# A hybrid conv/SSD and dilated-attention block pair in fp32: output scaling moved behind the hybrid projection, attention products regrouped

## The chip, the cores and the metric

The kernel runs on one core of one Trainium2 chip. The metric is device time in microseconds (us) of one execution. Data come in as fp32; no host arithmetic. A core's engines are TensorE (PE, with its weight loads as PEld), VectorE (DVE), ScalarE (ACT), GpSimd (POOL) and SyncE (SP, which issues the transfers here).

## The reference

A sequence of 256 tokens of width 1024 goes through two layers. Each layer is a half-step SwiGLU feed-forward block, a mixer, and another half-step feed-forward block, every one between two RMS norms. The mixer of layer 0 is a causal convolution joined with a state-space scan; that of layer 1 is attention over three patterns of eight heads.

```python
for i in range(DEPTH):
    h = h + 0.5 * rms_norm(swiglu(rms_norm(h, g[0]), w1[i, 0], w2[i, 0]), g[1])
    u = rms_norm(h, g[2])
    m = conv_ssd_mixer(u, ...) if i % 2 == 0 else dilated_attention_mixer(u, w_qkv, w_o)
    h = h + rms_norm(m, g[3])
    h = h + 0.5 * rms_norm(swiglu(rms_norm(h, g[4]), w1[i, 1], w2[i, 1]), g[5])

def conv_ssd_mixer(u, ...):
    conv_in, z, xbc, dt_raw = jnp.split(u @ w_in, [s0, s1, s2], axis=-1)
    ya = conformer_conv(conv_in, ...)      # 31-tap causal convolution, layer norm, silu
    yb = mamba2_ssd(z, xbc, dt_raw, ...)   # 4-tap convolution, chunked scan, silu(z) gate, rms_norm
    return jnp.concatenate([ya, yb], axis=-1) @ w_out

def dilated_attention_mixer(u, w_qkv, w_o):
    qkv = (u @ w_qkv).reshape(b, seq, 3, 3, 8, 64)
    for g, (window, dilation) in enumerate(((128, 1), (512, 4), (2048, 16))):
        o, l = dilated_window_attention(q[g], k[g], v[g], slopes, window, dilation)
        outs.append(o); lses.append(l)     # output and log-sum-exp of its scores, per group
    weights = softmax(stack(lses), axis=0)
    return einsum('gblh,gblhd->blhd', weights, stack(outs)).reshape(b, seq, 512) @ w_o
```

The norm at the end of `mamba2_ssd` divides each token's row by its root mean square over all 1024 channels and multiplies by a gain per channel. The merge of the three attention groups is a softmax over all three groups' scores at once.

## The kernel before, in words

Everything stays on the chip; tokens are two tiles (t = 0, 1) of 128 rows. Every dense product is done in three: a value is split into a high part rounded to the matmul's fp32r type and a low part (value minus high part), and hi x hi, hi x lo and lo x hi are added up in PSUM (`mm3`). Attention's scores and weighting are plain fp32 matmuls instead, which the trace and the order show as two passes each.

The 178 weight units of 1 MB come in one order (`_ffn_units`, `_hyb_units`, `_attn_units`): feed-forward 33 units (0 to 32), hybrid 26 (33 to 58), two feed-forward blocks, attention 20, feed-forward. `prefetch` runs three units ahead over four buffers each of `raw`, `wh`, `wl`: SP loads `raw`, ACT casts it to the high part `wh`, and DVE subtracts to get `wl`. For the units in `GPSIMD_UNITS` POOL does that subtraction instead, in pieces of `POOL_PIECE` columns, and ACT's cast is cut alike.

The hybrid stage computes the projections, DVE and ACT do the 31-tap convolution tap by tap, the scan works on PE with help from DVE, ACT and POOL, and its gated result sits in the tiles `v` (list `xs`, four of them, two halves per token tile). For each token tile `rstd` takes the row sums of squares, a power on POOL, and gives the row scale; the four v tiles are scaled on ACT, transposed on PE and split while they leave PSUM (`spread`, where the gain per channel is put in). Then the output projection collects in four PSUM banks `acc`: four units of products with the scan's part (`of_yb`), then four with the convolution's (`of_ya`).

The attention stage computes values of groups 0 and 1, then for each group q and k (feature-major, in `cv` tiles, both through the two "w" banks), the scores (64 features on one half of the array's rows per head, so that heads go in pairs on both halves), a running maximum and sum, and the exponentials. `weigh` for the group before transposes the probabilities (stationary operand, 128x128) and multiplies them with 64 columns of v; each group's output is added to `num`, rescaled by the change of the maximum. At the end `num` is divided by the sum, transposed, split and projected.

Every operation is recorded first (`Recorder`), and `schedule` then fixes the static order of each engine and the places of the buffers: among the operations that could start, by a modelled time (`cost`, `latency`), it takes the one of lowest rank, where the rank is the place in the program plus what `moved` adds. All operations are issued from one line, L423, so the profile's rows are told apart by tile names: wh and wl are a unit's high and low part, x transposed activations, a, w, t, c the four kinds of PSUM bank (4, 2, 1 and 1 of them), s scratch tiles in SBUF, cv the convolution's tiles and attention's q and k, v values, y0 and y1 half rows of 512, m small columns.

## Time and profile before

| what | value |
|---|---|
| three runs | 1132.56 us median, 1129.19 to 1132.75 |
| profiled execution | 1132.12 us, span 1130.3 us |
| PE busy | 1095.5 us of the span (97%), 5830 instructions |
| PEld, DVE, ACT, POOL busy | 919.5, 738.6, 635.2, 148.2 us |
| granted TensorE clock, mean | 0.993 |
| hybrid stage | from about 209 to 406 us |
| attention stage | from about 782 to 944 us |

Times in a view are us from the span's start. An instruction's row reads: its line, engine, operation, output <- inputs, shape and type, and its count. In a table of groups there follow the busy time, the mean of one in ns, and the idle time of the engine just before them with what ended it. The order of inputs in a PE row is moving operand first, stationary second. PE rows are pipelined, so that one's end runs on under the next; what a product costs on PE is read from start to start.

### The profile page before, as it was taken

The page shows a single profiled execution, that of the slowest core. Times are in us where ns is not written, and L with a number is a line of the kernel's source. Part 1 is how long each engine was busy: PE and PEld are TensorE (multiplying, and loading weights), DVE is VectorE, ACT ScalarE, POOL GpSimd, SP SyncE. Part 2 cuts the span into 40 slices and gives each one's busy share as a digit, 9 for nine tenths or more (in the row PEclk, how much of TensorE's full clock was granted, in tenths as well). Part 3 has the DMA queues.
Part 4 walks back from the last instruction along what each step waited for, and adds up shares of the span by engine and source line. Part 5 has one row for each costly group of instructions (what it writes and reads, how often), then busy time and mean ns, then how long its engine had stood idle before and what let it go on. Part 6 is the DMA issues. An engine that isn't in the chain of part 4 may idle for free.

```text
span 1130.3 us, 15336 instructions
## 1 busy us (share of the span) xinstructions
PE 1095.5 (97%) x5830; PEld 919.5 (81%) x5830; DVE 738.6 (65%) x1248; ACT 635.2 (56%) x1217; POOL 148.2 (13%) x200
## 2 busy tenths in 40 slices
PE   6999999999899999999999999999999999999997
PEld 5888888798767778888878888888877877888885
DVE  5756556799797685655686555667575657555563
ACT  7645545788667564554565454545565456455452
POOL 0000000379795300000010000001000000000000
PEclk9999999999999999999999999999999999999999
DMA  9755454534333466546546546554632424654521
GB/s 349 260 189 186 165 208 149 190 146 150 112 109 116 186 229 217 186 157 215 186 149 224 205 174 221 180 193 159 237 138 79 150 75 152 220 181 174 215 83 38
DMA packets 30203, 196.55 MB, mean 174 GB/s; under 512 B 3633, under 2 KB 4529, under 8 KB 7601
## 3 DMA queue, kind: packets, MB, share of 16 engines
q1 hardware_dynamic: 30128, 195.57, 48.9%
q8 instruction: 45, 0.74, 0.2%
q14 instruction: 30, 0.24, 0.1%
HBM read 194.51 MB, written 1.05 MB: 173 GB/s over the span
## 4 chain that ended last, share of the span: by engine, by line
PE 63%; DVE 4%; ACT 3%; POOL 3%; issue 1%; DVEq 0%; POOLq 0%; ACTq 0%
PE w L423 26%; PE a L423 22%; PE t L423 8%; PE c L423 7%; ACT s L423 1%; POOL wl L423 1%; ACT wh L423 1%; DVE y L423 1%; POOL s L423 1%; DVE wl L423 1%; DVE s L423 1%; POOL m L423 1%; DVE h L423 1%; DVE x L423 0%; DVE m L423 0%
## 5 line engine op out<-in xcount | busy, mean ns | idle before, releaser
L423 DVE TENSOR_TENSOR wl<-raw,wh 128x1024 fp32r<-128x1024 f32 (+1 forms) x322 | 385.1, 1220 | 215.6 <-ACT wh L423 214.0
L423 ACT ACTIVATE wh<-raw 128x1024 fp32r<-128x1024 f32 (+2 forms) x466 | 375.7, 854 | 232.4 <-PE a L423 91.5
L423 PE MATMUL w<-x,wh 128*128 128x512 f32 (+1 forms) x992 | 315.6, 373 | 3.5 <-DVE cv L423 2.1
L423 PE MATMUL w<-x,wl 128*128 128x256 f32 x880 | 247.9, 282 | 0.0
L423 PE MATMUL a<-wh,s 128*128 128x512 f32 x768 | 246.2, 395 | 0.0
L423 PEld LDWEIGHTS w<-x,wh 128*128 128x128 f32 x992 | 179.8, 189 | 40.2 <-DVE cv L423 3.1
L423 PEld LDWEIGHTS a<-wh,s 128*128 128x128 f32 x768 | 143.9, 188 | 34.7 <-DVE s L423 0.6
L423 PEld LDWEIGHTS w<-x,wl 128*128 128x128 f32 x880 | 166.9, 190 | 1.9 <-issue 0.6
L423 PE MATMUL w<-wh,x 128*128 128x512 f32 x480 | 159.3, 405 | 2.5 <-ACT x L423 2.5
L423 PE MATMUL a<-wl,s 128*128 128x512 f32 x384 | 151.8, 395 | 1.8 <-POOL wl L423 1.8
L423 POOL TENSOR_TENSOR m<-m,mhalf 128x1 f32<-128x1 f32 x28 | 19.6, 701 | 939.0 <-DVE m L423 939.0
L423 PEld LDWEIGHTS w<-wh,x 128*128 128x128 f32 x480 | 90.9, 191 | 24.6 <-ACT x L423 3.1
L423 POOL TENSOR_TENSOR wl<-raw,wh 128x256 fp32r<-128x256 f32 x144 | 103.7, 761 | 37.1 <-ACT wh L423 37.0
L423 PE MATMUL t<-x,wh 128*128 128x512 f32 x288 | 102.7, 396 | 0.0
L423 PE MATMUL c<-x,wh 128*128 128x512 f32 x288 | 102.7, 395 | 0.0
L423 PE MATMUL w<-wl,x 128*128 128x512 f32 x240 | 95.5, 400 | 1.7 <-POOL wl L423 1.7
L423 PEld LDWEIGHTS a<-wl,s 128*128 128x128 f32 x384 | 72.1, 188 | 17.6 <-POOL wl L423 2.2
L423 ACT ACTIVATE sg<-w 128x256 f32<-128x256 f32 x96 | 36.6, 382 | 86.7 <-PE w L423 86.6
L423 PE MATMUL t<-x,wl 128*128 128x256 f32 x288 | 80.8, 281 | 0.0
L423 PE MATMUL c<-x,wl 128*128 128x256 f32 x288 | 80.8, 281 | 0.0
L423 DVE TENSOR_TENSOR sg<-w,sg 128x256 f32<-128x256 f32 x72 | 30.3, 421 | 72.6 <-ACT sg L423 72.6
L423 PEld LDWEIGHTS t<-x,wh 128*128 128x128 f32 x288 | 54.0, 188 | 12.8
(167 smaller groups left out, 1211.3 us busy)
## 6 DMA issues: line engine op xcount, KB each, us to landing
raw<-in_weights SPq DMA_DIRECT2D x176, 1024.0 KB, 4.8
g<-in_gains SPq DMA_DIRECT2D x11, 512.0 KB, 4.7
raw<-in_weights SPq DMA_DIRECT2D x4, 256.0 KB, 6.1
raw<-in_weights SPq DMA_DIRECT2D x2, 512.0 KB, 7.9
out<-h SPq DMA_DIRECT2D x4, 256.0 KB, 2.1
s<-in_consts SPq DMA_DIRECT2D x3, 192.0 KB, 4.0
h<-in_x SPq DMA_DIRECT2D x2, 256.0 KB, 2.8
h<-in_x SPq DMA_DIRECT2D x1, 512.0 KB, 6.7
```

Source lines behind the costliest of these rows:

```text
L423: o.ins = f(*[real(a) for a in o.args], **{k: real(a) for k, a in o.kw.items()})
```

## The change

Hybrid stage. The v tiles are transposed and split without the row scale; the scale is kept (`rms`) and applied to the four PSUM accumulators, in place on ACT, when the scan's part of the projection is complete and before the convolution's part is added. POOL's pieces are 512 columns wide instead of 256, and unit 55 is split by DVE. In the planner, POOL's lengths are other numbers.

Attention stage. Group 2's values come first, those of groups 0 and 1 last. All three groups' scores are computed and exponentiated one after the other, with the products of a block put into one unbroken run by the new `together`; q goes through the "w" banks and k through "t" and "c". The probabilities of all groups are kept. `settle` brings those of groups 0 and 1 to the last maximum by multiplying them on POOL (12 tiles of 128x512 with a broadcast factor). `weigh` has v's 64 columns as the stationary operand and the transposed probabilities (128 columns) moving, heads by turns on the left and right half of the array's columns, and one accumulator per token tile takes all three groups. Evictions of transposed probabilities go to ACT and DVE by turns. The result is already transposed; the reciprocal sums are spread out and transposed instead (`spread`), multiplied in, and the product is split for the projection. Line 423 becomes line 439.

```diff
-POOL_PIECE = 256
+POOL_PIECE = 512
-GPSIMD_UNITS = range(38, 56)
+GPSIMD_UNITS = range(38, 55)
...
-SMALL = {1: 16, 2: 12, 8: 12, 12: 2, 16: 6, 32: 8}
+SMALL = {1: 16, 2: 12, 8: 28, 12: 2, 16: 6, 32: 8}
...
+    def together(self):
+        at = len(self.ops)
+        yield
+        head, rest = self.ops[at], self.ops[at + 1 :]
+        for o in rest:
+            for d, read in o.deps.items():
+                if d < at:
+                    head.deps[d] = head.deps.get(d, False) or read
...
+            o.rank = head.rank - RUN
+            o.deps.setdefault(o.index - 1, False)
...
+        if PAIRED and (stationary.ap.ap[0][1] == 64 or stationary.free_size() == 64):
+            return max(2 * n / 2.4 + 5.0, 110.0), 0.0
...
-        return (2.35 if out.ap.dtype == F32R else 1.9) * n + 40.0, 0.0
+        spread = any(isinstance(v, View) and v.ap.ap[-1][0] == 0 for v in kw.values())
+        return (1.95 if spread else 2.35) * n + (10.0 if spread else 92.0), 0.0
...
-            r = self.rstd(ss, EPS)
-            for g in range(2):
-                nc.scalar.activation(xs[t][g], xs[t][g], AF.Copy, scale=r)
+            rms.append(self.rstd(ss, EPS))
...
-                out_unit(of_yb, j, t, units[j], j == 0, False)
+                out_unit(of_yb, j, t, units[j], j == 0, j == 3)
+
+            for half in acc[t]:
+                nc.scalar.activation(half, half, AF.Copy, scale=rms[t])
...
+                for n, s in enumerate(probs[t][g]):
+                    i, r = n // 2, n % 2
+                    nc.gpsimd.tensor_tensor(out=s, in0=s, in1=fv[:, i * per : (i + 1) * per, r].unsqueeze(2).to_broadcast([P, per, (t + 1) * P]), op=ALU.mult)
...
+                if i % 2:
+                    V.tensor_copy(out=o, in_=ps)
                 else:
+                    nc.scalar.activation(o, ps, AF.Copy)
...
+                with nc.together():
+                    blocks = [divmod(n, nb) for n in range(4 * i, 4 * i + 8)]
+                    for kb in range(nb):
+                        for hd in sorted({hd for hd, _ in blocks}):
+                            n = hd * nb + kb
+                            out = po[t][(hd % 2) * 64 : (hd % 2) * 64 + 64, hd // 2, :]
+                            nc.tensor.matmul(out, v[kb][:, hd * 64 : (hd + 1) * 64], pT[n // 4][:, n % 4, :], start=g == 2 and kb == 0 and hd < 2, stop=g == 1 and kb == nb - 1 and hd >= 6)
...
+        v = values(2)
+        for g in range(3):
+            softmax(g, proj(0.125, "ww"), proj(1.0, "tc"))
+        rden = [settle(t) for t in range(NT)]
+        for t in range(NT):
+            weigh(2, t, v)
+        for g in range(2):
+            v = values(g)
+            for t in range(NT):
+                weigh(g, t, v)
+            if g == 0:
+                rden = [spread(t, rden[t]) for t in range(NT)]
```

The order of the engines, at three places. A row gives the line, the operation, output <- inputs (moving, stationary; the number at a name's end is the buffer's own), shape and count. First PE in the hybrid stage, where the products with unit 48 (wh_48, wl_48) go into accumulator a_22. Before:

```order
L423 MATMUL a_22_2945<-x_6_1718,wh_48_2822 128x256 x2
L423 MATMUL a_22_2945<-x_6_1718,wl_48_2860 128x256
L423 MATMUL a_22_2945<-x_6_1718,wh_48_2822 128x256 x2
L423 MATMUL w_36_2828<-wh_46_2581,x_7_1721 128x512
L423 MATMUL a_22_2945<-x_6_1718,wl_48_2860 128x256
L423 MATMUL a_22_2945<-x_7_1721,wh_48_2822 128x256 x2
L423 MATMUL w_36_2828<-wl_46_2645,x_7_1721 128x512
L423 MATMUL w_36_2828<-wh_46_2581,x_7_1721 128x512
L423 MATMUL a_22_2945<-x_7_1721,wl_48_2860 128x256
L423 MATMUL a_22_2945<-x_7_1721,wh_48_2822 128x256 x2
L423 MATMUL w_37_2989<-wh_45_2487,x_4_1710 128x512
L423 MATMUL a_22_2945<-x_7_1721,wl_48_2860 128x256
```

and now:

```order
L439 MATMUL a_22_2858<-x_5_1714,wh_48_2738 128x256 x2
L439 MATMUL a_22_2858<-x_5_1714,wl_48_2793 128x256
L439 MATMUL a_22_2858<-x_6_1718,wh_48_2738 128x256 x2
L439 MATMUL w_36_2747<-wl_46_2586,x_7_1721 128x512
L439 MATMUL w_36_2747<-wh_46_2516,x_7_1721 128x512
L439 MATMUL w_37_2885<-wh_45_2433,x_4_1710 128x512
L439 MATMUL w_37_2885<-wl_45_2520,x_4_1710 128x512
L439 MATMUL w_37_2885<-wh_45_2433,x_4_1710 128x512 x2
L439 MATMUL w_38_2895<-x_4_1710,wh_47_2661 128x256 x2
L439 MATMUL w_38_2895<-x_4_1710,wl_47_2725 128x256
L439 MATMUL w_38_2895<-x_4_1710,wh_47_2661 128x256 x2
L439 MATMUL w_38_2895<-x_4_1710,wl_47_2725 128x256
```

The products of a_22 were mixed with three of w_36. Now a_22 stops in its third quarter of channels (x_6), and two products of w_36, four of w_37 and 24 of w_38 (wh_47, wl_47, in rows like the last four to x_7) come before the first one that reads wl_48 again.

Second, PE where the transposes of v begin and the scan's part of the output projection (a_35, a_36 with unit 51) follows. Before:

```order
L423 MATMUL w_41_3223<-wh_50_3064,x_7_1721 128x512 x2
L423 MATMUL w_41_3223<-wl_50_3072,x_7_1721 128x512
L423 MATMUL w_43_3435<-ident_0_70,cv_13_2832 128x128 x2
L423 MATMUL w_43_3435<-ident_0_70,cv_14_2853 128x128 x2
L423 MATMUL w_41_3223<-wh_50_3064,x_7_1721 128x512
L423 MATMUL w_44_3466<-ident_0_70,v_0_2891 128x128 x4
L423 MATMUL w_45_3476<-ident_0_70,v_2_3184 128x128 x4
L423 MATMUL a_35_3489<-wh_51_3138,x_8_3482 128x512
L423 MATMUL a_35_3489<-wl_51_3165,x_8_3482 128x512
L423 MATMUL a_36_3498<-wh_51_3138,x_8_3482 128x512
```

and now:

```order
L439 MATMUL w_41_3246<-wh_50_3001,x_6_1718 128x512
L439 MATMUL w_44_3307<-ident_0_70,v_0_2807 128x128 x4
L439 MATMUL w_41_3246<-wh_50_3001,x_7_1721 128x512
L439 MATMUL w_41_3246<-wl_50_3013,x_7_1721 128x512
L439 MATMUL w_41_3246<-wh_50_3001,x_7_1721 128x512 x2
L439 MATMUL w_41_3246<-wl_50_3013,x_7_1721 128x512
L439 MATMUL w_41_3246<-wh_50_3001,x_7_1721 128x512
L439 MATMUL a_35_3330<-wh_51_3036,x_8_3318 128x512
L439 MATMUL a_35_3330<-wl_51_3071,x_8_3318 128x512
L439 MATMUL a_36_3336<-wh_51_3036,x_8_3318 128x512
L439 MATMUL a_36_3336<-wl_51_3071,x_8_3318 128x512
L439 MATMUL a_35_3330<-wh_51_3036,x_8_3318 128x512
```

The first transposes of v (w_44) came after the last product of w_41 (the z gate) and with those of w_45; now w_44 stands five rows of w_41 earlier, and w_45 and w_46 between the projection's products.

Third, PE in the attention stage, scores of the first group's second half of heads (cv_36 to cv_38) into the banks a_47 to a_52. Before:

```order
L423 MATMUL w_108_7525<-x_20_7100,wh_133_7360 128x512
L423 MATMUL w_108_7525<-x_20_7100,wl_133_7371 128x256
L423 MATMUL w_108_7525<-x_20_7100,wh_133_7360 128x512
L423 MATMUL w_108_7525<-x_20_7100,wl_133_7371 128x256
L423 MATMUL w_108_7525<-x_21_7104,wh_133_7360 128x512
L423 MATMUL w_108_7525<-x_21_7104,wl_133_7371 128x256
L423 MATMUL a_51_7541<-cv_38_7482,cv_36_7388 128x256 x2
L423 MATMUL w_108_7525<-x_21_7104,wh_133_7360 128x512
L423 MATMUL w_108_7525<-x_21_7104,wl_133_7371 128x256
L423 MATMUL w_108_7525<-x_22_7108,wh_133_7360 128x512
L423 MATMUL a_52_7554<-cv_38_7482,cv_36_7388 128x256 x2
```

and now:

```order
L439 MATMUL a_47_7303<-cv_38_7260,cv_36_7166 128x128
L439 MATMUL a_48_7305<-cv_38_7260,cv_36_7166 128x128
L439 MATMUL a_47_7303<-cv_38_7260,cv_36_7166 128x128
L439 MATMUL a_48_7305<-cv_38_7260,cv_36_7166 128x128
L439 MATMUL w_102_7287<-x_21_6952,wl_131_7149 128x256
L439 MATMUL w_102_7287<-x_22_6956,wh_131_7138 128x512
L439 MATMUL a_51_7321<-cv_38_7260,cv_36_7166 128x256
L439 MATMUL a_52_7324<-cv_38_7260,cv_36_7166 128x256
L439 MATMUL a_51_7321<-cv_38_7260,cv_36_7166 128x256
L439 MATMUL a_52_7324<-cv_38_7260,cv_36_7166 128x256
L439 MATMUL w_102_7287<-x_22_6956,wl_131_7149 128x256
L439 MATMUL w_102_7287<-x_22_6956,wh_131_7138 128x512
```

The two 256-wide products on a_51 stood together, and those on a_52 four projection products later; now a_51 and a_52, on the two halves of the array's rows, go by turns without a break.

More of the change, by code (lines that the diff above doesn't have):

```diff
@@ L428 @@
 GAP = 100.0
+PAIRED = True
 FIRST = 730.0
@@ new lines, in spread @@
+        def spread(t, r):
+            wide = self.slot([P, 8, 64], tag="cv")
+            nc.scalar.activation(wide, r.unsqueeze(2).to_broadcast([P, 8, 64]), AF.Copy)
+            wide = wide.rearrange("p h c -> p (h c)")
+            ps = self.ps([P, 4, P], "tc"[t])
+            for b in range(4):
+                nc.tensor.transpose(ps[:, b, :], wide[:, b * P : (b + 1) * P], self.ident)
+            out = self.slot([P, 4, P], tag=f"y{t}")
+            nc.scalar.activation(out, ps, AF.Copy)
+            return out
```

191 lines of the change are left out of this document (91 added, 100 removed).

## The prediction

> **What bounds the kernel now.** I read the stage windows first, then the waits of TensorE (PE) in the two stages that the diff touches, then the single gaps, then the groups by shape. The other four stages are the two half-steps' feed-forward work, which the diff leaves alone. The stages read: start:end, length, then busy time and count of PE, PEld, DVE, ACT and POOL, the granted clock, the DMA share and GB/s.
>
> ```profile
> 209.00:406.00 197.00, 185.19 (x1082) 155.22 (x1081) 163.59 (x394) 136.79 (x346) 133.38 (x174) 0.98 0.41 146
> ...
> 594.00:782.00 188.00, 187.77 (x961) 157.66 (x960) 118.10 (x163) 99.05 (x160) 3.04 (x4) 1.00 0.55 193
> 782.00:944.00 162.00, 155.63 (x909) 130.37 (x908) 102.52 (x198) 93.72 (x223) 3.03 (x4) 0.99 0.38 136
> ```
>
> A feed-forward stage (second row) has PE busy for 187.8 of 188 us. The hybrid stage (first row) leaves it 11.8 us idle, the attention stage (third) 6.4. DMA is busy for 0.41 and 0.38 of the time, so weights arrive in time in both. PE is the bound, and time can only come from its idle time, its clock, and what its instructions cost. POOL, idle elsewhere, works 133 of 197 us in the hybrid stage. PE's waits there (total, times, longest):
>
> ```profile
> PE a L423 <- POOL wl L423: 4.6, 2, 2.8
> PE w L423 <- ACT v L423: 2.4, 1, 2.4
> PE w L423 <- POOL wl L423: 1.7, 1, 1.7
> ...
> PE a L423 <- POOL s L423: 0.8, 1, 0.8
> ```
>
> and in the attention stage:
>
> ```profile
> PE w L423 <- DVE cv L423: 2.1, 1, 2.1
> PE t L423 <- ACT s L423: 1.3, 2, 1.0
> ```
>
> The long ones in the timeline of PE (start, length, work, and in brackets the idle time before it), and, last, two products in undisturbed work:
>
> ```profile
> 295.77 0.49 PE L423 MATMUL a<-x,wl 128*128 128x256 f32 x1 [2.81 <-POOL wl L423]
> ...
> 343.12 0.55 PE L423 MATMUL w<-ident,v 128*128 128x128 f32 x3 [2.41 <-ACT v L423]
> ...
> 375.87 0.50 PE L423 MATMUL a<-wl,s 128*128 128x512 f32 x1 [1.80 <-POOL wl L423]
> ...
> 872.19 0.50 PE L423 MATMUL w<-x,wh 128*128 128x512 f32 x1 [2.14 <-DVE cv L423]
> ...
> 818.12 0.39 PE L423 MATMUL w<-x,wh 128*128 128x512 f32 x1
> 818.35 0.28 PE L423 MATMUL w<-x,wl 128*128 128x256 f32 x1
> ```
>
> From start to start a 512-wide product takes 0.23 us; half as wide is 0.12.
>
> A long gap costs twice. Of the four windows of 3.40 us below, three start right behind the gaps of 2.81, 2.41 and 2.14 us, and the last lies in undisturbed work; the third number from the end is the granted clock.
>
> ```profile
> 295.90:299.30 3.40, 3.40 (x13) 3.01 (x14) 0.00 (x0) 1.04 (x2) 1.19 (x2) 0.50 0.30 96
> 343.70:347.10 3.40, 3.40 (x11) 2.73 (x11) 3.25 (x12) 3.40 (x12) 2.42 (x4) 0.50 0.01 2
> 872.75:876.15 3.40, 3.40 (x12) 2.86 (x11) 1.23 (x1) 1.10 (x2) 0.00 (x0) 0.50 0.03 2
> 100.00:103.40 3.40, 3.40 (x21) 3.01 (x20) 0.95 (x2) 1.88 (x3) 0.00 (x0) 1.00 0.26 106
> ```
>
> At half clock 3.4 us of work is 1.7 us late, so each of these three gaps costs its idle time plus 1.7: 4.5, 4.1 and 3.8 us.
>
> **Hybrid: POOL's splits in halves instead of quarters.** POOL works out the low parts of units 38 to 55 in 128x256 pieces; now of 38 to 54, in 128x512. The rows of POOL, and a stretch of its timeline ahead of the first gap:
>
> ```profile
> L423 POOL TENSOR_TENSOR wl<-raw,wh 128x256 fp32r<-128x256 f32 x144 | 103.7, 761 | 37.1 <-ACT wh L423 37.0
> ...
> L423 POOL TENSOR_TENSOR v<-v,y 128x512 f32<-128x512 f32 x4 | 5.2, 1300 | 0.0
> ...
> 279.13 11.90 POOL L423 TENSOR_TENSOR wl<-raw,wh 128x256 fp32r<-128x256 f32 x17
> 290.99 2.04 POOL L423 TENSOR_TENSOR s<-v,m 128x512 f32<-128x512 f32 x2
> ```
>
> A quarter goes by at 11.90/17 = 0.70 us. For a half with its fp32r result no row exists: below, it costs the 1.30 of v<-v,y, which reads two tiles of that size; above, two quarters, 1.40. I take 1.30, the row of the same size. 144 x 0.70 = 100.8 becomes 68 x 1.30 = 88.4, so POOL is done 12 us sooner: 7 us from the 68 wider pieces (0.10 each), and 5.6 us (8 x 0.70) from unit 55, whose two 1.2 us pieces go to DVE. A coarser piece also makes the first quarter's reader wait up to 0.6 us more.
>
> What PE gains: at 295.77 it waited for unit 48's low part. In the new order 30 products with operands long there (units 45 to 47) stand ahead of that point; 24 of them 256 wide at 0.12 and 6 of them 512 wide at 0.23, 4.3 us, more than the 2.81 missing. So 4.5 goes. The 1.65 and 0.8 us waits for POOL are shorter than what POOL gains by then: 2.4 goes. The 1.80 us wait is for unit 55, now on DVE, which in the same stretch has its convolutions behind it: 1.8 goes.
>
> **Hybrid: the scaling moved behind the output projection.** Four ACT scalings of v, and the wait for the norm they need, leave the path to the transposes; four in-place scalings of PSUM halves come in.
>
> ```profile
> 341.75 0.56 POOL L423 TENSOR_TENSOR m<-m,mhalf 128x1 f32<-128x1 f32 x1
> ...
> L423 ACT ACTIVATE v<-v,m 128x512 f32<-128x512 f32 x4 | 2.7, 740 | 0.0
> ...
> L423 ACT ACTIVATE s<-a 128x512 f32<-128x512 f32 x10 | 5.6, 608 | 1.5 <-PE a L423 1.5
> ```
>
> The wait of 2.41 us ended with ACT's v; without the power on POOL (0.56) and two scalings (2 x 0.7), and with a transpose now placed among w_41's products, it is covered: 4.1 goes. The new scalings have no row: from 0 (if they replace what they remove) to 0.6 each beyond. They take 0.61 by the row that reads PSUM, 2.4 in all for 2.7 removed. Behind them on ACT stand the casts of the next units and, for the second token tile, they stand behind eight silu halves; who waits is PE's first ya product of that tile. Token tile 0's pair lies under tile 1's yb products, 48 of 0.23; tile 1's under tile 0's ya products, 12 of 0.23 = 2.8 us for 1.2. I cost them at nothing; uncovered, they are 2.4.
>
> **What is late next.** The sum so far is 4.5 + 2.4 + 1.8 + 4.1 = 12.8. But the ya products need DVE's convolution, whose end the gaps do not set.
>
> ```profile
> 354.42 0.48 DVE L423 SCALAR_TENSOR_TENSOR cv<-cv,chan,c 128x256 f32<-128x256 f32 x1
> ...
> 365.07 0.76 DVE L423 TENSOR_TENSOR s<-pt,s 128x256 fp32r<-128x256 f32 x2 [0.76 <-ACT s L423]
> ...
> 371.56 0.40 PE L423 MATMUL a<-wh,s 128*128 128x512 f32 x1
> ```
>
> From the end of the convolutions at 354.9 to a usable half of ya at 365.8 it is 10.9 us, and PE used it first at 371.56, so it has 5.8 us of slack. PE would now come 11.0 us earlier (12.8 less the 1.8 after it). DVE itself wins about 4 (it idles while PE waits at 295), minus up to 2.4 for unit 55: between 2 and 4. So PE waits 11.0 - 5.8 - 2..4 = 1 to 3 us there. Hybrid: 12.8 - 3 = **10**.
>
> **Attention: products with the values stationary.** The groups of PE in that stage:
>
> ```profile
> L423 PE MATMUL a<-v,s 128*128 128x64 f32 x144 | 16.7, 273 | 0.0
> ...
> L423 PE MATMUL a<-cv,cv 64*128 64x256 f32 x48 | 9.9, 398 | 0.7 <-DVE s L423 0.7
> ...
> L423 PE MATMUL a<-cv,cv 64*128 64x128 f32 x48 | 4.5, 297 | 0.9 <-DVE cv L423 0.9
> ...
> 852.63 3.68 PE L423 MATMUL a<-v,s 128*128 128x64 f32 x32
> 856.25 2.92 PE L423 MATMUL a<-cv,cv 64*128 64x128 f32 x22
> ...
> 818.91 1.80 PE L423 MATMUL a<-cv,cv 64*128 64x128 f32 x20
> ...
> 823.52 1.13 PE L423 MATMUL a<-cv,cv 64*128 64x256 f32 x4 [0.17 <-DVE s L423]
> 824.58 0.51 PE L423 MATMUL w<-x,wh 128*128 128x512 f32 x1
> ```
>
> Probabilities by values: 32 passes take 3.62 us to the next row's start, 0.11 each for 64 columns. The same 144 passes remain, with 64 stationary and 128 moving columns, on the array's left and right column halves by turns. No row has column halves. Row halves have one: four unpaired score passes of 256 took 1.06 (823.52 to 824.58), about 0.215 each with 0.2 for the change of form; 128 columns are then 0.11. The 20 passes at 818.91, 8 of 256 and 12 of 128 (their shapes apart, the view gives x8 and x12), would take 3.0 one by one and took 1.8. So different parts of the array do run side by side. Bounds for the 144: side by side 72 x 0.11 = 7.9; one by one 144 x 0.11 = 15.8. To either come some 18 changes of form at 0.1, 1.8. I take side by side, as the row halves show it: 15.9 (144 x 0.11) becomes 9.7, and 6.2 goes. The Trainium skill, "TensorE: Matmul & The Clock Gate", section "Measured speedup vs the span model", reports 2.38 times for three column tiles, about four fifths of ideal. By that the passes take some 9.9 instead of 7.9 as an estimate, and the sum would be 2 us worse.
>
> **Attention: scores in runs.** 48 passes of 256 and 48 of 128 take 14.4 by the rows. All paired they take 24 x 0.215 + 24 x 0.11 = 7.8, with some 17 changes of form 9.5. A row's busy time holds the 0.07 that a group's last pass runs on under the next work (1.13 against 1.06), 0.8 over a dozen groups, so 4.1 goes. If the runs break up again, nothing.
>
> **Attention: banks, settling, order.** q's products go to the two "w" banks and k's to "t" and "c", so that k no longer waits for q's eviction: of the 872.19 wait 3.8 goes. The wait of 1.3 for ACT's s is shared between ACT and DVE now. New are 12 POOL products of 128x512, the rescaling of groups 0 and 1; the nearest row is the 1.05 of s<-v,m (2.04 for 2), up to 1.30: 12.6 to 15.6 us. They lie beside two values projections, 96 products of 0.23 = 22 us, and group 2's weighting. I cost them at nothing; without that cover they would be 13. Loads follow the new unit order, as many as before, with DMA at 0.38. For new waits at the banks I take off 1: attention 6.2 + 4.1 + 3.8 - 1 = **13**.
>
> **The sum.** From the profiled execution's 1132.1 (span 1130.3 and 1.8 around it) 10 + 13 = 23 leaves 1109; the median of the runs is 0.4 higher. **1110**, alone between 1103 (PE waits nowhere new) and 1117 (3 us more lost in each stage).
>
> **Rivals.**
> (1) Column halves take turns. No row shows them side by side; the row halves speak for it. The products then lose 1.7 (17.6 for 15.9) where the sum has them win 6.2: 7.9 worse, **1118**. Chance 0.13.
> (2) The convolution sets the hybrid stage's end: DVE wins nothing and gets unit 55 too. PE then waits 11.0 - 5.8 + 2.4 = 7.6 for ya and the stage saves 5: **1115**. For it speaks DVE's 163.6 busy us of 197, against it its idle 4 us at 295. Chance 0.17; with (1), another 0.03, at 1122.
> (3) POOL's settling is held up by DVE. Two rows of a stage change:
>
> ```profile
> 402.74 1.39 POOL L423 TENSOR_TENSOR m<-m,mhalf 128x1 f32<-128x1 f32 x1 [3.84 <-DVE m L423]
> 402.52 1.21 DVE L423 TENSOR_TENSOR wl<-raw,wh 128x1024 fp32r<-128x1024 f32 x1
> ```
>
> A power of 0.56 took 1.39 and ended 0.4 after DVE's split did: POOL stood while that split ran. The two values projections bring four units, eight such splits of 1.2 = 10 us. Settling then takes 13 + 10 = 23 against a cover of 22 that starts late; I price it at 5, **1115**. Chance 0.06. "GPSIMD Engine Reference", section "Key points" of the Trainium skill, says the same: POOL contends with VectorE instructions that have two SBUF inputs; the two rows agree.
> (4) Slower: the half pieces on POOL cost far more than the quarters. Place: the splits of units 38 to 54; POOL then bounds the hybrid stage. To turn the attention stage's 13 over, POOL's work must grow by 13 and by the 37.1 us that it idles ahead of its splits, 50/68 = 0.74 a piece: from 2.1 us on it decides whatever else happens. At 2.4 it is 68 - 37 - 13 = 18 slower, **1150**. Against it: 1.30 in v<-v,y. Chance 0.03.
> (5) The change does not do what it says: scheduled on other waits than seen, both stages keep their idle time and the products' 10 us are lost to new waits: about **1132**. Chance 0.03.
>
> **Chances and range.** The forecast has 0.55. Faster than by 0.3% (3.4 us, about what a measurement here tells from no change) are forecast and rivals 1 to 3, 0.94, less 0.02 for their mixtures: 0.92; same 0.04; slower 0.04. The range, from the forecast's own 1103 and the DVE slack fully used below (1100) to both of (1) and (2) above (1123), leaves out under 2 in 10.
>
> **What would show it.** Right: no PE gap over 1 us with POOL wl or ACT v behind it, clock 1.00 through the hybrid stage; 128x512 wl on POOL near 1.30; a PE gap of 1 to 3 us ahead of the first ya product; attention's 64x128 passes 0.055 us apart; its 256-wide scores 0.11; POOL's 12 products done before their transposes. Wrong: passes 0.11 apart (rival 1), a long wait for DVE's s (2), PE waiting for POOL's s (3), halves of 2 us (4).

## The result, and the profile after

The changed kernel takes 1104.07 us (median of 4 runs, 1103.48 to 1104.48) against 1131.97 for the kernel before in the same session: a ratio of 0.9757, interval 0.9739 to 0.9775. That is 28 us less; the forecast was 1110, 22 less than before, within 1100 to 1123. Run again beside other kernels it took 1104.97 against 1131.93 (0.9765, 0.9751 to 0.9780), 27 less.

The stage windows of the changed kernel (same columns as before; boundaries moved with the work):

```profile
209.00:395.00 186.00, 183.75 (x1088) 154.03 (x1088) 165.03 (x399) 130.08 (x270) 116.56 (x98) 1.00 0.45 156
583.00:771.00 188.00, 185.66 (x950) 155.52 (x949) 117.89 (x162) 99.64 (x160) 3.04 (x4) 1.00 0.54 187
771.00:917.00 146.00, 143.64 (x903) 116.56 (x903) 106.58 (x193) 89.39 (x212) 17.06 (x16) 1.00 0.43 152
```

PE is idle for 2.3 us in the hybrid stage (11.8 before) and 2.4 in the attention stage (6.4), and the clock is 1.00 in both. New is what the second row shows: the last microseconds of the feed-forward stage ahead of attention hold 2.3 us of idle PE, where before there was 0.2.

PE's waits in the hybrid stage of the changed kernel, whole list (total, times, longest):

```profile
PE w L439 <- DVE pt L439: 0.7, 1, 0.7
PE w L439 <- DVE s L439: 0.5, 2, 0.3
PE c L439 <- DVE pt L439: 0.2, 1, 0.2
PE t L439 <- DVE y L439: 0.2, 1, 0.2
PE a L439 <- ACT s L439: 0.2, 1, 0.2
PE a L439 <- ACT v L439: 0.2, 1, 0.2
```

No wait for POOL is left, nor the one for the scaled v. In the attention stage:

```profile
PE c L439 <- DVE cv L439: 0.9, 1, 0.9
PE t L439 <- ACT cv L439: 0.6, 1, 0.6
PE w L439 <- ACT x L439: 0.4, 1, 0.4
PE t L439 <- DVE y L439: 0.4, 2, 0.2
```

The wait for k's eviction is gone; two short ones for evictions of transposed probabilities are new. The groups of PE there that were costed, and one run of weighting with its neighbours in the timeline:

```profile
L439 PE MATMUL a<-cv,cv 64*128 64x256 f32 x48 | 6.8, 402 | 0.0
...
L439 PE MATMUL a<-cv,v 128*64 128x128 f32 x96 | 6.6, 279 | 0.0
...
L439 PE MATMUL a<-cv,cv 64*128 64x128 f32 x48 | 3.5, 285 | 0.0
L439 PE MATMUL a<-cv,y 128*64 128x128 f32 x48 | 3.3, 279 | 0.0
```

```profile
868.78 1.09 PE L439 MATMUL a<-cv,v 128*64 128x128 f32 x16
869.80 0.50 PE L439 MATMUL w<-wh,x 128*128 128x512 f32 x1
```

Sixteen passes of 128 columns take 1.02 us to the next start, 0.064 each. Inside the nine such runs a pass starts 0.055 us after the one before it; the rest is the change of form at a run's end, where the last pass lasts 0.20 us until the next work starts. POOL's groups:

```profile
L439 POOL TENSOR_TENSOR wl<-raw,wh 128x512 fp32r<-128x512 f32 x68 | 85.7, 1291 | 25.0 <-ACT wh L439 24.0 <-ACT x L439 0.8 <-issue 0.2
...
L439 POOL TENSOR_TENSOR s<-s,m 128x512 f32<-128x512 f32 x14 | 16.1, 1182 | 99.1 <-ACT m L439 98.9
```

A half piece takes 1.29 us. Twelve of the 14 in the second row are the rescaling.

Where the time went is best seen stage by stage. All kernels here have 5830 PE instructions, the untouched stages in the same order, so the start of the 1000th, 2100th, 3900th, 4900th and 5800th PE instruction marks the same places in every trace (just ahead of the hybrid stage, behind it, ahead of the attention stage's start, behind it, near the end). Lengths between them, in us, worked out from the traces of all kernels of this study:

```
                 to 1000  hybrid  2 ffn   attention  ffn    rest   span
before           207.6    201.2   349.6   182.6      174.9  14.5   1130.3
before, again    206.9    200.8   349.6   182.6      174.9  14.5   1129.3
changed          206.2    188.5   349.0   170.5      174.3  13.3   1101.8
changed, again   207.1    188.5   349.0   170.5      174.3  13.3   1102.7
hyb_only         207.0    188.5   349.1   181.7      174.9  13.4   1114.6
attn_only        207.4    203.1   349.7   171.6      174.6  13.4   1119.7
scale_only       206.3    196.4   348.3   182.7      174.4  13.4   1121.5
old_lengths      207.5    190.3   349.2   171.7      174.8  13.8   1107.2
pieces256        207.9    194.0   348.0   170.3      174.3  13.8   1108.2
one_half         207.4    188.5   349.0   173.3      174.3  13.3   1105.7
same_half        207.2    188.6   349.1   179.2      174.3  13.3   1111.7
no_runs          207.2    188.4   349.0   175.5      174.8  13.7   1108.5
two_first        206.8    188.8   349.0   175.5      174.4  13.4   1107.8
late_split       207.6    188.4   349.0   168.8      174.3  13.3   1101.4
```

The hybrid stage gave 12.5 us (10 forecast) and the attention stage 12.1 (13 forecast). Another 2.3 lie outside both, 0.6 in each of the two feed-forward parts and 1.1 behind the last products.

The 12.1 us of the attention stage are made up as follows, from start to start of PE's instructions. The weighting gains 6.7 us and the scores 3.9. The projections and transposes around them lose 2.2 (147.24 us for 145.06), about 1.5 of it because the product ahead of a run lasts some 0.1 us longer than it does elsewhere (865.01 to 865.34 in the first run of weighting, for 0.23). PE's idle time falls by 2.0 (4.4 for 6.4), and the 1.7 lost at half clock are gone.

### The profile page after: what moved, and what is told of

Same layout as the page of the kernel before. It is cut to its first block, busy times and chain, and to the rows that moved or that the text cites. A ratio compares the mean times of both kernels' runs of the same rounds, so it can differ in the third digit from the quotient of the medians.

```text
span 1101.8 us, 15214 instructions
## 1 busy us (share of the span) xinstructions
PE 1080.2 (98%) x5830; PEld 903.6 (82%) x5830; DVE 745.2 (68%) x1251; ACT 625.9 (57%) x1136; POOL 145.4 (13%) x136
## 4 chain that ended last, share of the span: by engine, by line
PE 88%; DVE 7%; ACT 2%; issue 1%; POOL 1%; DMA 0%; SPq 0%; DVEq 0%; POOLq 0%; ACTq 0%
PE w L439 34%; PE a L439 31%; PE t L439 12%; PE c L439 12%; DVE c L439 1%; DVE t L439 1%; DVE y L439 1%; ACT wh L439 1%; DVE wl L439 1%; POOL m L439 1%; DVE h L439 1%; DVE x L439 1%; DVE s L439 1%; DMA gain<-in_chan 0%; DVE m L439 0%
## 5 line engine op out<-in xcount | busy, mean ns | idle before, releaser
L439 ACT ACTIVATE wh<-raw 128x1024 fp32r<-128x1024 f32 (+1 forms) x392 | 368.5, 978 | 223.9 <-PE a L439 93.4
L439 PE MATMUL w<-x,wh 128*128 128x512 f32 (+1 forms) x896 | 279.3, 368 | 0.9 <-DVE pt L439 0.7
L439 PE MATMUL w<-x,wl 128*128 128x256 f32 x784 | 220.8, 282 | 0.0
L439 PEld LDWEIGHTS w<-x,wh 128*128 128x128 f32 x896 | 160.8, 188 | 31.6 <-DVE pt L439 1.0
L439 PEld LDWEIGHTS w<-x,wl 128*128 128x128 f32 x784 | 148.0, 189 | 2.6 <-issue 0.9
L439 PE MATMUL c<-x,wh 128*128 128x512 f32 x336 | 119.6, 395 | 0.0
L439 PE MATMUL t<-x,wh 128*128 128x512 f32 x336 | 119.4, 394 | 0.0
L439 PE MATMUL t<-x,wl 128*128 128x256 f32 x336 | 94.2, 280 | 0.0
L439 POOL TENSOR_TENSOR wl<-raw,wh 128x512 fp32r<-128x512 f32 x68 | 85.7, 1291 | 25.0 <-ACT wh L439 24.0
L439 PEld LDWEIGHTS c<-x,wh 128*128 128x128 f32 x336 | 63.0, 188 | 14.8
```

Source lines behind the costliest of these rows:

```text
L439: o.ins = f(*[real(a) for a in o.args], **{k: real(a) for k, a in o.kw.items()})
```

## The experiments

**The two halves of the change apart.** One kernel has the hybrid half with the attention stage of before, the other the reverse (unit order, functions and constants each with its half).

```diff
 hyb_only:  attention, _attn_units of before; PAIRED = False; 8: 12 in SMALL
 attn_only: hybrid of before; POOL_PIECE = 256; GPSIMD_UNITS = range(38, 56); POOL lengths of before
```

> The hybrid half of the change alone, with the attention stage of before. If the two halves are independent, this one is worth what the two traces show between the start of the hybrid stage and the start of the next, 12.7 us: about 1119, and the attention stage keeps its wait of 2.1 us for k's eviction with the half clock behind it. If the halves lean on each other (the attention stage starts on another phase, its units come from other buffers), the two single kernels' gains will not add up to the 28 of the whole, by more than 3 us.

> The attention half alone, with the hybrid stage of before. Independent halves: 12.2 us less than before by the traces, about 1120, with the waits of 2.8, 2.4 and 1.8 us in the hybrid stage back at full length, each of the first two with its 3.4 us of half clock. Halves that lean on each other: off by more than 3 us.

Measured in one session, before at 1132.29: hyb_only 1117.92 (ratio 0.9873, 0.9858 to 0.9888), 14.4 less; attn_only 1119.70 (0.9880, 0.9859 to 0.9900), 12.6 less. Together 27.0 against 27 to 28 for the whole: the halves add up. The table shows it too, 188.5 for the hybrid stage with either attention stage. The attention stage alone shows that a gap's price is not fixed: in hyb_only the old wait for k's eviction stands at full length,

```profile
858.49 0.50 PE L440 MATMUL w<-x,wh 128*128 128x512 f32 x1 [2.12 <-DVE cv L440]
```

but the clock stayed up behind it, so the stage took 181.7 instead of 182.6; in attn_only the hybrid stage took 203.1 instead of 201, since 6.8 us instead of 3.4 ran at half clock behind its first gap. More on that in the last section.

**Scaling alone.** The kernel before with only the scaling behind the projection.

```diff
-            r = self.rstd(ss, EPS)
-            for g in range(2):
-                nc.scalar.activation(xs[t][g], xs[t][g], AF.Copy, scale=r)
+            rms.append(self.rstd(ss, EPS))
...
+            for half in acc[t]:
+                nc.scalar.activation(half, half, AF.Copy, scale=rms[t])
```

> The kernel before, with only the scaling moved behind the output projection; POOL's pieces, units and lengths as before. If the wait of 2.4 us for ACT's v came from the norm alone, it goes with its 1.7 us of half clock, and the rest of the stage stays: about 1128. If POOL was late there in any case (its gated products come from the same engine that is behind with splits), PE waits for POOL in its place: 1131 to 1133.

It took 1123.18 against 1132.32 (0.9925, 0.9910 to 0.9940), 9.1 less, more than either expectation. By its trace the hybrid stage accounts for 4.4 to 4.8 of them. PE's waits there:

```profile
PE a L423 <- POOL wl L423: 2.9, 1, 2.9
PE w L423 <- POOL wl L423: 1.7, 1, 1.7
...
PE w L423 <- ACT s L423: 0.6, 1, 0.6
```

The wait of 2.41 for ACT's v has become one of 0.64 for another operand, and its half clock is gone. The first row held two waits before and holds one now: the 1.8 us wait for unit 55 went as well, although that unit is still split by POOL in quarters. In this order POOL does two of unit 55's eight pieces ahead of the silu work on ACT, where before it did none:

```profile
357.86 1.43 POOL L423 TENSOR_TENSOR wl<-raw,wh 128x256 fp32r<-128x256 f32 x2 [0.69 <-ACT wh L423]
```

The in-place scaling, which had no row in the kernel before, takes 0.67 us a half (four in 2.6). The other 4 us of its gain lie in stages that it does not touch (1.3 in the two feed-forward parts, 0.5 and 1.1 at the end, about 1 ahead of the stage); what causes those differences was not found.

**What POOL's numbers are worth.** Two kernels undo one part each of the POOL side: the planner's lengths, and the width of the pieces.

```diff
 old_lengths:
-        spread = any(isinstance(v, View) and v.ap.ap[-1][0] == 0 for v in kw.values())
-        return (1.95 if spread else 2.35) * n + (10.0 if spread else 92.0), 0.0
+        return (2.35 if out.ap.dtype == F32R else 1.9) * n + 40.0, 0.0
 pieces256:
-POOL_PIECE = 512
+POOL_PIECE = 256
```

> The changed kernel, planned with the old lengths for POOL; pieces of 512, the moved scaling and the attention stage stay. In PE's order the products of unit 48 stand in one block again, with no work of other units between them. If what emptied the wait of 2.8 us at unit 48 is that the planner knows how long POOL takes and puts other work there, the wait is back with its half clock, and the weighting's start may meet POOL late too: 3 to 5 us slower than the change, 1107 to 1109. If it is POOL's shorter work with wider pieces, the wait stays away: 1104.

> The changed kernel with POOL's pieces 256 wide as before (units 38 to 54, 136 pieces), planned with the true lengths. POOL's splits take 136 x 0.70 = 95 instead of 86 us. If knowing the lengths is what counts, PE's order makes room for them (in it, the block of unit 48 is broken earlier than in the change) and the time stays within 1 us: 1104 to 1105. If the 9 us that wider pieces save on POOL carry the gain, the waits for POOL's wl are back in part: 1107 or more.

Before was at 1131.93 and the changed kernel at 1104.97 in that session. old_lengths took 1107.80 (0.9788, 0.9772 to 0.9804). Its hybrid stage is 1.8 us longer, and its attention stage 1.2, which is half clock behind the gap at that stage's start and none of POOL's doing. The wait at unit 48 did **not** return, though PE's order has unit 48's products in one block again; the longest waits of its hybrid stage are these:

```profile
PE w L439 <- ACT y L439: 0.8, 1, 0.8
PE w L439 <- DVE pt L439: 0.7, 1, 0.7
PE a L439 <- POOL s L439: 0.5, 1, 0.5
```

pieces256 took 1110.02 (0.9810, 0.9796 to 0.9825), 5 us more than the change. Its hybrid stage is 5.5 us longer, mostly from one wait of 3.25 us with half clock behind it (in the window below, 0.50):

```profile
329.76 0.50 PE L439 MATMUL w<-wl,x 128*128 128x512 f32 x1 [3.25 <-POOL wl L439]
```

```profile
330.90:334.30 3.40, 3.40 (x10) 2.62 (x9) 3.40 (x10) 0.00 (x0) 3.40 (x6) 0.50 0.98 412
```

The product that waits reads unit 50; it is the one that waited 1.65 us in the kernel before. So at unit 48 either cure is enough, the wider pieces or the order; behind it, at unit 50, only the wider pieces keep POOL in time. Knowing the true lengths is worth the 1.8 us by which the hybrid stage of old_lengths is longer. pieces256 came out as its second expectation has it. old_lengths came out as neither: its time lies where the wait's return was expected, but that wait stayed away, and other, shorter waits and a window of half clock in the attention stage gave the time.

**Whether column halves run side by side.** In one_half a run's products are sorted, left half first; in same_half all products of a run lie on one half, so that the heads' results land in the wrong places. Order and shapes of the PE instructions are otherwise the change's.

```diff
 one_half:
-                        for hd in sorted({hd for hd, _ in blocks}):
+                        for hd in sorted({hd for hd, _ in blocks}, key=lambda h: (h % 2, h)):
 same_half:
-                            out = po[t][(hd % 2) * 64 : (hd % 2) * 64 + 64, hd // 2, :]
+                            side = int(g == 0) if t == 0 else hd // 4
+                            out = po[t][side * 64 : side * 64 + 64, hd % 4, :]
...
```

> The changed kernel, with the weighting products of a run sorted so that all products on the left column half come first and then all on the right; number, shapes and place of the runs stay. If the gain of the weighting is that two column halves work side by side, its 144 passes go back from 0.064 to about 0.11 us, 6.6 us more: about 1111. If it came from the roles of the operands (64 values stationary, 128 columns moving) or from the runs alone, the order within a run changes nothing: about 1104.

> The changed kernel, with all products of a weighting run on one column half (the left for one run, the right for another; the heads' results then lie in the wrong places, so the output is not the reference's). The order of the instructions is the same. If column halves side by side are the gain, the 9 runs of 16 passes take 16 x 0.11 = 1.76 us instead of 1.09, 6 us in all: about 1110. The run with one half after the other had 1.58 in three runs and 1.15 in six: if that was not overlap across several passes but some other cost, this one shows the same 1.15 to 1.58, 1104 to 1108.

one_half took 1107.58 (0.9782, 0.9767 to 0.9796), 3.5 more than the change and not the 6.6 expected; by the table 2.8 of it in the attention stage, 1.0 of which is half clock ahead of the weighting. Runs of token tile 0, where eight passes on one half are followed by eight on the other, take 1.51 us from start to start (867.56 to 869.07):

```profile
867.56 1.58 PE L439 MATMUL a<-cv,v 128*64 128x128 f32 x16
869.07 0.66 PE L439 MATMUL t<-ident,s 128*128 128x128 f32 x4
```

Runs of token tile 1, where the sides change after four passes, have a busy time of 1.15 against 1.09. So work on the other half need not be next in line to overlap. same_half settles it: 1112.78 (0.9829, 0.9813 to 0.9845), about 8 more than the change, with all nine runs at 1.89 us (867.43 to 869.32):

```profile
867.43 1.96 PE L439 MATMUL a<-cv,v 128*64 128x128 f32 x16
869.32 0.66 PE L439 MATMUL t<-ident,s 128*128 128x128 f32 x4
```

0.118 a pass on one half, 0.064 on both: a factor of 1.85. Both figures hold the change of form at a run's end; inside the runs a pass starts 0.113 us after the one before it on one half and 0.055 on both, a factor of 2. The 144 passes cost 17.0 on one half and 9.2 as they are, 7.8 us apart; the other 0.9 by which this kernel's attention stage is longer come with a window of half clock at its start, as in one_half. With one half the new weighting would be slower than the old one (15.9).

**Whether the runs make the pairs.**

```diff
-                    with nc.together():
+                    with nc.moved(0):
...
-                with nc.together():
+                with nc.moved(0):
```

> The changed kernel without the rule that keeps the products of a block together, for scores and weighting alike; operands, halves and lengths stay. If the runs make the pairs, the scores go back from 9.7 us towards the 13.6 of before and the weighting loses part of its 6.7: about 1108 to 1111. If PE finds its pairs anyway, over several instructions, nothing is lost: 1104 to 1105.

1110.95 (0.9815, 0.9800 to 0.9829), 6 to 7 more. The attention stage is 5.0 us longer. Its score groups are back at nearly their old size:

```profile
L439 PE MATMUL a<-cv,cv 64*128 64x256 f32 x48 | 9.9, 389 | 0.0
...
L439 PE MATMUL a<-cv,cv 64*128 64x128 f32 x48 | 4.3, 297 | 0.0
```

From start to start the scores take 12.8 instead of 9.7 and the weighting 9.8 instead of 9.2, 3.8 together; the last 1.2 fall on the projections between the pieces, where the changes of form end up. What came apart in the scores is the 256-wide work of the second half of heads. Four passes on one half of the array's rows, then two projection products, then the four passes on the other half:

```profile
801.00 1.13 PE L439 MATMUL a<-cv,cv 64*128 64x256 f32 x4
...
802.61 1.13 PE L439 MATMUL a<-cv,cv 64*128 64x256 f32 x4
```

Each four take 1.06 us to the next start, as long as all eight take by turns in the changed kernel. With two products between them the halves did not overlap; the passes that this order left by turns still did.

**The cover, and the new wait at the attention stage's start.** two_first brings the values of group 1 forward beside those of group 2, as two groups were before.

```diff
-        v = values(2)
+        v, v1 = values((2, 1))
...
-        for g in range(2):
-            v = values(g)
+        for t in range(NT):
+            weigh(1, t, v1)
+        rden = [spread(t, rden[t]) for t in range(NT)]
+        v = values((0,))[0]
```

> The changed kernel with values of groups 2 and 1 both ahead of the scores (24 more products for token tile 0 at the stage's start) and group 0's alone behind them. By the account of the traces the wait of 2.25 us at the stage's start goes, since 24 products of 0.23 lie there instead. Against it: half the projections that POOL's 14 us of rescaling lie beside are gone, since the values of group 1 are already there. If that cover is needed, PE waits for POOL's s or for evictions in the weighting for some 5 to 10 us and the kernel is slower than the change, 1107 to 1112; if the rescaling had room to spare, about 1102.

1109.98 (0.9803, 0.9789 to 0.9818), 5.9 slower than the change. The gap at the start is gone, as expected, and the lost cover shows elsewhere:

```profile
PE t L440 <- ACT cv L440: 3.1, 5, 1.1
PE c L440 <- DVE cv L440: 2.6, 3, 1.8
PE a L440 <- ACT s L440: 1.2, 1, 1.2
```

None of these is for POOL's rescaling. By these waits, what the values projections hide in the first place is the way of each probability tile from the transpose through an eviction to the weighting.

late_split leaves the order of the values alone and holds two DVE splits (units 127 and 128) back until DVE has scaled token tile 1 for the attention stage, by a dependency that the planner sees.

```diff
...
+        for u in (127, 128):
+            for n in self.splits[u]:
+                self.nc.ops[n].deps.setdefault(self.scaled[9], False)
         self.nc.issue()
```

> The changed kernel, with the DVE splits of units 127 and 128 held back until DVE has scaled token tile 1 for the attention stage. In the changed kernel PE stands for 2.25 us at the stage's start while two splits of 1.2 us lie among the six DVE steps it waits for, one of them keeping POOL's power waiting too. If that is the cause, 1.1 and about 0.85 us go, the wait is 0.3 us and the kernel 2 us faster than the change: about 1102. If the chain waits for ACT's sums of squares instead, or the split that is late now holds up q's products, no gain: 1104 or more.

The cause is in DVE's timeline of the changed kernel ahead of the gap, with two splits among the steps that PE waits for and a longer wait for POOL's power behind the second:

```profile
760.00 1.22 DVE L439 TENSOR_TENSOR wl<-raw,wh 128x1024 fp32r<-128x1024 f32 x1
761.13 1.41 DVE L439 SCALAR_TENSOR_TENSOR h<-y,m,h 128x512 f32<-128x512 f32 x2
762.46 1.29 DVE L439 TENSOR_TENSOR y<-h,g 128x512 f32<-128x512 f32 x2
763.66 0.21 DVE L439 TENSOR_SCALAR m<-m 128x1 f32<-128x1 f32 x1
763.78 1.22 DVE L439 TENSOR_TENSOR wl<-raw,wh 128x1024 fp32r<-128x1024 f32 x1
765.44 0.88 DVE L439 TENSOR_SCALAR y<-y,m 128x512 f32<-128x512 f32 x2 [0.44 <-POOL m L439]
```

The kernel before has the same split and the same slow power at this place,

```profile
778.42 1.22 DVE L423 TENSOR_TENSOR wl<-raw,wh 128x1024 fp32r<-128x1024 f32 x1
```

```profile
778.65 1.40 POOL L423 TENSOR_TENSOR m<-m,mhalf 128x1 f32<-128x1 f32 x1 [3.83 <-DVE m L423]
```

but there 33 products of the values projections lie ahead of the transposes, 7.7 us, instead of 24, 5.6 us, and PE waits for only 0.21. POOL's power in the change and then in late_split:

```profile
764.02 1.39 POOL L439 TENSOR_TENSOR m<-m,mhalf 128x1 f32<-128x1 f32 x1 [3.83 <-DVE m L439]
```

```profile
764.47 0.55 POOL L439 TENSOR_TENSOR m<-m,mhalf 128x1 f32<-128x1 f32 x1 [2.92 <-DVE m L439]
```

PE's wait in the change, and in late_split:

```profile
766.08 0.30 PE L439 MATMUL t<-ident,y 128*128 128x128 f32 x1 [2.25 <-DVE y L439]
```

```profile
765.68 0.63 PE L439 MATMUL t<-ident,y 128*128 128x128 f32 x4 [0.53 <-DVE y L439]
```

The mechanism is shown: 1.7 us less of wait, and an attention stage of 168.8 instead of 170.5. In the runs it is 1103.59 (1102.95 to 1103.73; ratio 0.9748, 0.9734 to 0.9763), the lowest median of all kernels here. Against the two sessions of the change, 1104.07 and 1104.97, the intervals of the ratios overlap, so a gain of about 1 us is likely but not settled by the times.

**The same kernels again**, for traces from one chip.

> The kernel before, once more, for a trace from the same chip as the others. In the first trace of before and that of the change the two stages account for 24.9 of 28.5 us; 1.4 lie ahead of the first stage's end (the clock came up after 16.0 us there and after 13.8 in the change), 1.2 in the untouched feed-forward stages, 1.1 at the end. If that rest is the phase of the clock's windows and differences between executions, this trace shows other numbers there, the hybrid and attention stages the same. If it is the kernel, it shows the same.

> The changed kernel, once more, beside the others on the same chip. 1104 within 1 us, with the same wait of 2.25 us at the start of the attention stage; the clock's first rise somewhere between 13 and 17 us.

before again took 1131.91 (1.0000, 0.9991 to 1.0009), the changed kernel 1104.97. The 1.4 us ahead of the hybrid stage did not repeat (206.9 and 207.1), so that part was chance. The 0.6, 0.6 and 1.1 us in the untouched parts did repeat. Kernels that change only one half show some of them and not others (hyb_only 349.1, 174.9, 13.4), so they don't follow one part of the change. PE's idle time in the two feed-forward parts is the same 0.2 us in both kernels, so the 0.6 lie in how closely the products follow one another; the 1.1 lie behind DVE's last operation, while the output is written. Their cause stays open.

## Why the prediction held, point by point

**What bounds.** PE, with time to be won only from idle time, clock and the products' own cost: held. The 24.6 us of the two stages are all of these kinds.

**Unit 48, 4.5 us: right in size, too narrow in cause.** The two traces part by about 4.4 at this place. The prediction gave it to the new order of PE; old_lengths shows that wider pieces alone do it, pieces256 that the order alone does.

**The 1.65 and 0.8 waits for POOL, 2.4 us: right.** They are gone, and pieces256 shows that the wider pieces carry this term: without them a wait of 3.25 with half clock stands at the product that had waited 1.65. The price of 1.30 a half piece, taken from a row of another operation, measured 1.29.

**The wait for scaled v, 4.1 us: right.** scale_only alone turns 2.41 us and half clock into 0.64, and the change leaves nothing there. The in-place scalings cost 0.67 each and no PE time that shows.

**Unit 55, 1.8 us: gone, but the reason given is not shown.** The prediction had it go because DVE does the split; in scale_only it goes with the split still on POOL, so moving the scaling is enough. Which of the two acts in the change was not tested apart.

**A wait of 1 to 3 us for the convolution's part: wrong.** This is the step that mis-sized the hybrid stage. The convolution's end and the first product with ya in the changed kernel:

```profile
347.48 0.48 DVE L439 SCALAR_TENSOR_TENSOR cv<-cv,chan,c 128x256 f32<-128x256 f32 x1
...
350.45 1.23 DVE L439 TENSOR_TENSOR wl<-raw,wh 128x1024 fp32r<-128x1024 f32 x1
```

```profile
359.34 0.50 PE L439 MATMUL a<-wh,s 128*128 128x512 f32 x1 [0.20 <-ACT s L439]
```

The convolution ended at 348.0 instead of 354.9, 7 us earlier, 5.6 without the 1.4 of the stage's start. The prediction allowed 2 to 4: it counted DVE's wait of 4 us at 299 alone, and put unit 55's splits ahead of that end. The wait went as forecast, shorter waits of DVE behind it shrank too (its waits of over 0.3 us up to that end add up to 9.3 instead of 14.6), and the planner put the splits behind the end (350.45). PE then came 12.2 us earlier (359.34 for 371.56), 10.8 without that 1.4, and waited 0.20. Slack of 5.8 and a gain of 5.6 cover this almost exactly, so rival 2 was close: by this sum, one DVE split of 1.2 more in that stretch would have been seen.

**Weighting, 6.2 us: right.** 15.9 became 9.2 from start to start, 6.7. Inside the runs a pass takes the 0.055 that was forecast, 7.9 in all; 1.3 are the changes of form at the runs' ends, and those at their beginnings, some 0.1 each, fall on the work ahead. Rival 1 would have cost 7.9; same_half puts the difference at 7.8. The Trainium skill's page "TensorE: Matmul & The Clock Gate", section "Measured speedup vs the span model", with its 2.38 for three column tiles, would have given some 9.9 for the passes alone by the estimate in the prediction; they came out at 7.9, a factor of 2 for two halves, and at 9.2 with the changes of form behind them.

**Scores, 4.1 us: right.** 13.6 became 9.7, 3.9, and no_runs gives 3.2 of it back. But the two product terms together, 10.3 forecast, brought 8.4 and not 10.6 to the stage, because the projections and transposes between the runs lost 2.2.

**k's eviction, 3.8 us: right for this trace.** The half clock behind such a gap comes in some executions and not in others, as hyb_only shows, so 2.1 is certain and 1.7 is not.

**Settling at nothing: right.** POOL did its twelve products in 14.0 us, and PE waited for none.

```profile
864.33 14.02 POOL L439 TENSOR_TENSOR s<-s,m 128x512 f32<-128x512 f32 x12 [98.92 <-ACT m L439]
```

Rival 3 did not happen. Its mechanism is at work at another place, as it was in the kernel before: POOL's power at the attention stage's start took 0.84 us longer with a DVE split under way (1.39 for 0.55). Rival 4's price starts from a half piece of 1.40, where the sum has 1.30; that changes nothing here.

**One us for new waits: the long one was not seen.** The wait of 2.25 at the stage's start comes from the step "values of group 2 first": 24 products ahead of token tile 1's transposes where there had been 33, and the missing nine are 2.1 us; two_first, which puts products back there, has no such gap. The prediction counted the values projections as cover for POOL at the stage's end and forgot what they covered at its start. On balance the 1 us was not even needed: apart from the wait for k, PE's idle time in the stage is 4.4 us after 4.2 before, as new waits took the place of old ones. Rivals 4 and 5 did not happen.

**The sum.** 12.5 + 12.1 for 10 + 13, with 2.3 outside that no term had: 26.9 for the 23 of the sum. In the hybrid stage the term that was mis-sized is the wait for the convolution's part (3 taken off, 0.2 measured), 2.5 too little gain. In the attention stage two errors in part cancel: the products brought 1.9 less than forecast, and the new waits cost 0.9 less on balance than the 1 taken off. That this stage came within 0.9 of its sum is partly luck. The 2.3 have no explanation, and the last us or so is scatter between executions.

## What to carry to other kernels

When work is moved from the start of a stage to its end, count what it covered where it stood as well as what it will cover. Matmuls that use half of the array paid here only beside a partner on the other half, and the partners had to stand close: they overlapped less with eight passes between them, and not at all with two projection products between. Check the pass time from start to start (0.055 paired, 0.113 alone here) rather than the busy row, and count what the change of form adds to the work on both sides of a run. And where one engine is late for several readers, as POOL was here, a better order hid the first wait only, while shorter work on that engine removed all of them.

## What the runs showed of the hardware

A gap's price in clock depends on where it falls. In every trace the half-clock stretches lie on a grid of 3.41 us that starts with the clock's first rise, which comes anywhere from 13.8 to 16.9 us into the span. Over the fourteen traces, up to PE's last product, every window in which PE was idle for 0.52 of the time or more was followed by half clock (15 of them), and none with 0.49 or less (the nearest six have 0.43 to 0.49). Behind the last product one trace departs from this: in hyb_only PE was idle for 0.56 of a window, and the clock fell one window later. The half clock lasted one window, and two in one case, in attn_only, where PE was idle for 0.7 us of the first of the two. The gap of 2.25 to 2.3 us at the attention stage's start shows both cases. In the changed kernel the clock rose at 13.77; the gap, 763.83 to 766.08, covers 0.25 of window 219 and 0.41 of window 220, and the clock stayed up. In one_half it rose at 16.36; the gap, 765.00 to 767.28, lies in one window, 0.67 of it, and this followed:

```profile
767.29:770.70 3.41, 3.41 (x12) 2.99 (x13) 2.88 (x7) 1.33 (x4) 0.00 (x0) 0.50 0.81 296
```

The Trainium skill's page "TensorE: Matmul & The Clock Gate", section "What's actually happening", describes a free-running window of 3413 ns; the grid agrees with it. It also names an idle window as the condition; here about half of one was enough, and the measurement decides. So a gap under 1.7 us never cost more than its own length in these traces, and a longer one costs some 1.7 us more in some executions and not in others.

Two more things were not expected. Passes on the other half of the array overlap even when four passes of the first stand between, though less when it is eight (1.51 us a run against 1.02). And a POOL operation on one column per partition took 1.39 us with a DVE split of 128x1024 under way, and 0.55 in late_split, where that split and one ahead of it come later.
